# Fills of 6, 9 and 9 products, a priority for the recurrence's steps, and the embedding moved ahead of the last two pool units

## The chip, the core and the metric

The kernel runs on one core of one Trainium2 chip. A core has a matmul engine (TensorE, in the profile PE, with PEld for its weight loads), a vector engine (DVE), a scalar engine (ACT), GpSimd (POOL) and SyncE (SP), which only issues DMA transfers here. Each engine works through its own list of instructions in order; semaphores tie the lists together. Transfers are issued by SP and ACT and run beside the engines. The metric is the time of one execution on the device, in microseconds (us).

## The reference

One layer of a decoder with 512 tokens and a width of 2048, in float32. Half of the width is a linear recurrence (RWKV-7, 16 heads of 64), the other half causal means over trailing windows of 2, 4, 8 and 16 tokens. The code is cut to what is computed; `token_shift` delays by one token.

```python
h = rms_norm(x, norm_g[i])
z = jnp.einsum('btd,dn->btn', h, w_in[i])
# columns of z: r, k, v, two low-rank inputs, gate of the heads, pool input u, gate of the pool
zs = zs + (token_shift(zs) - zs) * mu[i]
...
def step(S, inp):                      # the recurrence, token by token, for each head
    sa = jnp.einsum('bhvk,bhk->bhv', S, -kk_t)
    S = (S * w_t[:, :, None, :]
         + sa[..., None] * (kk_t * a_t)[:, :, None, :]
         + v_t[..., None] * k_t[:, :, None, :])
    y_t = jnp.einsum('bhvk,bhk->bhv', S, r_t)
    return S, y_t
...
y = head_group_norm(y, ln_w[i], ln_b[i])
y_rwkv = (y + bonus.reshape(B, T, D_RWKV)).astype(dt) * jax.nn.silu(g_rwkv)
d = causal_multiscale_pool(u).astype(dt)
y_pool = jnp.einsum('btgc,gcd->btgd', d, w_pool[i]).reshape(B, T, D_POOL)
y_pool = y_pool * pool_scale[i] * jax.nn.silu(g_pool)
x = x + jnp.einsum('btc,cd->btd', jnp.concatenate([y_rwkv, y_pool], axis=-1), w_out[i])
gate = jax.nn.sigmoid(jnp.einsum('btd,de->bte', x, w_pg[i]) + b_pg[i])
x = x + gate * jnp.einsum('btq,qd->btd', p[i], w_ple[i])
return rms_norm(x, final_g)
```

## The kernel before

**Precision and products.** Every large product is made of three: each operand is split into a high and a low part (L132, L133 for weights: ACT casts the high part, DVE subtracts to get the low one), and `mm3` issues high by high, high by low, low by high. A "product" below is one instruction with 512 columns.

**Stages.** Up to about 50 us x is normalised and transposed into `hhi`, `hlo`. Then, to about 712 us, eight pairs of heads (j = 0 to 7) are worked through by `recur(j)`. Until 750 us what is left of the filler runs out, then come the product with w_out (`acc_o`) and, from about 930 us, the one with w_pg (`acc_g`).

**A pair of heads.** `recur(j)` goes over 8 chunks of 64 tokens. A chunk is a chain of three steps, called hops here. In *py*, PE multiplies by the state `sbd`, and DVE adds into `zs` (L773). In *pu*, PE multiplies by `zs`, and ACT copies the result into `uv` in two halves (L781). In *ps*, PE multiplies by `uv`, and DVE writes the next state `sbd` in two halves (L790 in the first chunk, L792 behind it); POOL makes `s0p` from it. Each hop waits for the one ahead, so PE needs other work in between.

**The filler.** That work is a generator, `stream()`, over the list `jobs`: the columns k, r, v and g of the next pair (48 products each), 16 pool units (`pool_unit(n)`, 48 products `zb` each; units with n mod 4 of 0 or 1 make windowed sums by DVE, L409 to L413, the others a gate and the map `wp` of 6 products, `pp`), and the embedding p by w_ple (`embed_unit`, four of 24 products, `pple`; ACT copies each result into `ple` and stores it to `pled`, from where `recall` loads it later). `pump(n)` draws at least n products: the generator yields 3 at a time, and what was drawn too much is carried over in `debt`. Between hops stand `pump(HC1)`, `pump(HC2)`, `pump(HC3)` of 8 products each, so that with steps of three the fills come as 9, 9 and 6 in turn. In the first chunk `between()` draws 16 products, computes the scores of the next pair (`pbo`, `pm`) and draws 16 more. Behind the eight chunks `finish` (transposes `pyt`, gate, store of `yo` to `yd`) is put off into the next pair's `gather`; for the last pair it runs behind `pump(HE)` at the end. `load_y` reads `yd` back as `yin` and splits it into `yhi`, `ylo` for w_out, in the order 8 to 13, 0 to 7, 14, 15.

**What sets the order.** PE's order is that of the program text (`keep_in_program_order`) up to the end of the filler. On the other engines a scheduler orders the instructions by priority, which is the place in the program unless it is raised. Buffers come from pools in turn: an instruction that writes a tile waits until the last reader of that buffer is done, for `ple` until the store to `pled` has landed.

In head 7 the filler in the hops is pool units (the last drawn there is the beginning of unit 15), and the embedding stands at the end of `jobs`, behind unit 15.

## Time and profile before

| | us |
|---|---|
| time, median of 3 runs | 1123.82 (1123.53 to 1124.64) |
| the profiled execution | 1124.23 |
| its span | 1122.5 |
| PE busy in the span | 1080.7 |
| mean granted clock | 0.994 of full |

How to read it: a row of the timeline gives the start, the duration, the engine, the line, the operation with output and inputs, the shape, how many such instructions in a row, and in brackets how long the engine stood idle ahead of it and what released it. A row of the waits gives the engine, the tile and the line that waited, what it waited for, then the total, how often and the longest. Matmuls are pipelined and their ends are modelled, so that rows of PE overlap. Durations of all other engines are measured. The letters q and ld behind an engine (ACTq, SPq, PEld) are its issue of DMAs and its weight loads.

### The profile page before, as it was taken

To read this page: it belongs to the slowest core of one execution; us is meant where nothing else is said; L and a number is where in the kernel's file an instruction comes from. 1 tells how busy PE (TensorE), PEld (TensorE's weight loads), DVE (VectorE), ACT (ScalarE), POOL (GpSimd) and SP (SyncE) were. 2 spreads that over 40 slices of the span, in tenths; PEclk is the share of its full clock that TensorE was granted. 3 is DMA by queue.
4 is the path that set the end of the run, shared out by engine and by line. 5 is a ranking of instruction groups with operands and counts; after the bars stand their busy time and mean duration, and the time that the engine had idled before them with its cause. 6 is when DMAs were issued, how large, how long until landed. Compare 5 with 4: busy or idle time off the path is not lost.

```text
span 1122.5 us, 17255 instructions
## 1 busy us (share of the span) xinstructions
PE 1080.7 (96%) x6090; PEld 881.0 (78%) x6090; DVE 707.8 (63%) x1835; ACT 450.1 (40%) x917; POOL 68.5 (6%) x180
## 2 busy tenths in 40 slices
PE   5999999999999999999999999979999999999996
PEld 4888887877877877878778787857888888888885
DVE  6677868778679688687886946534424423345265
ACT  7633435335335244353352433453222222233246
POOL 2100110110010000200101002000000000000000
PEclk9999999999999999999999999989999999999998
DMA  7433333332423333324234342486434437354444
GB/s 227 118 90 96 103 102 78 104 92 73 122 75 103 101 85 91 98 68 113 76 98 118 88 119 66 133 282 231 161 101 162 139 125 226 112 188 147 143 132 150
DMA packets 178357, 138.56 MB, mean 123 GB/s; under 512 B 34549, under 2 KB 139614, under 8 KB 178270
## 3 DMA queue, kind: packets, MB, share of 16 engines
q1 hardware_dynamic: 158270, 104.94, 31.7%
q10 hardware_dynamic: 20000, 32.52, 9.0%
q8 instruction: 48, 0.79, 0.3%
q14 instruction: 39, 0.32, 0.1%
HBM read 118.02 MB, written 18.87 MB: 122 GB/s over the span
## 4 chain that ended last, share of the span: by engine, by line
PE 59%; DVE 8%; ACT 3%; DMA 3%; issue 2%; ACTq 0%; DVEq 0%
PE acc_o L156 15%; PE acc_g L156 14%; PE zb L156 12%; PE zg L156 4%; PE zk L156 4%; PE zr L156 2%; PE zv L156 2%; DMA pled<-ple 2%; PE py L156 1%; DVE xw L648 1%; DVE tm L644 1%; DMA yin<-yd 1%; PE pp L156 1%; PE pm L156 1%; PE pu L156 1%
## 5 line engine op out<-in xcount | busy, mean ns | idle before, releaser
L133 DVE TENSOR_TENSOR wlo_g<-raw_g,whi_g 128x512 fp32r<-128x512 f32 x88 | 59.4, 684 | 85.6 <-ACT whi_g L132 85.3
L156 PE MATMUL zb<-hhi,whi_b 128*128 128x512 f32 x256 | 108.0, 422 | 0.0
L133 DVE TENSOR_TENSOR wlo_o<-raw_o,whi_o 128x512 fp32r<-128x512 f32 x64 | 43.8, 691 | 98.3 <-ACT whi_o L132 97.7
L156 PE MATMUL acc_o<-whi_o,yhi 128*128 128x512 f32 x256 | 101.4, 396 | 4.2 <-issue 4.1
L132 ACT CAST whi_g<-raw_g 128x512 fp32r<-128x512 f32 x88 | 54.4, 621 | 117.9 <-PE acc_g L156 72.2
L156 PE MATMUL acc_o<-wlo_o,yhi 128*128 128x512 f32 x256 | 101.3, 396 | 0.4 <-DVE wlo_o L133 0.4
L156 PE MATMUL acc_o<-whi_o,ylo 128*128 128x512 f32 x256 | 101.2, 395 | 0.0
L156 PE MATMUL zb<-hhi,wlo_b 128*128 128x512 f32 x256 | 100.6, 393 | 0.0
L156 PE MATMUL zb<-hlo,whi_b 128*128 128x512 f32 x256 | 100.0, 390 | 0.0
L156 PE MATMUL acc_g<-whi_g,x2hi 128*128 128x512 f32 (+1 forms) x224 | 86.7, 387 | 0.0
L156 PE MATMUL acc_g<-wlo_g,x2hi 128*128 128x512 f32 (+1 forms) x224 | 86.3, 385 | 0.0
L156 PE MATMUL acc_g<-whi_g,x2lo 128*128 128x512 f32 x224 | 86.0, 386 | 0.0
L132 ACT CAST whi_o<-raw_o 128x512 fp32r<-128x512 f32 x64 | 39.7, 623 | 104.0 <-PE acc_o L156 97.9
L132 ACT CAST whi_b<-raw_b 128x512 fp32r<-128x512 f32 x64 | 39.7, 620 | 79.5 <-PE zv L156 34.5
L799 POOL TENSOR_SCALAR s0p<-sbd,pw 64x64 f32<-64x64 f32 x96 | 49.2, 513 | 341.7 <-DVE sbd L792 256.4
L133 DVE TENSOR_TENSOR wlo_b<-raw_b,whi_b 128x512 fp32r<-128x512 f32 x64 | 43.8, 686 | 34.2 <-ACT whi_b L132 31.6
L156 PEld LDWEIGHTS acc_o<-whi_o,yhi 128*128 128x128 f32 x256 | 48.7, 190 | 14.9 <-issue 4.5
L156 PEld LDWEIGHTS acc_o<-wlo_o,yhi 128*128 128x128 f32 x256 | 48.7, 190 | 11.8 <-DVE wlo_o L133 1.6
L156 PEld LDWEIGHTS zb<-hhi,wlo_b 128*128 128x128 f32 x256 | 48.0, 188 | 11.2
L156 PEld LDWEIGHTS acc_o<-whi_o,ylo 128*128 128x128 f32 x256 | 48.8, 191 | 9.9
L648 DVE TENSOR_TENSOR xw<-xw,tm 128x60 f32<-128x60 f32 (+24 forms) x248 | 52.0, 210 | 6.8
L156 PEld LDWEIGHTS zb<-hhi,whi_b 128*128 128x128 f32 x256 | 48.3, 189 | 8.5
(283 smaller groups left out, 2541.6 us busy)
## 6 DMA issues: line engine op xcount, KB each, us to landing
raw_b<-in_w_in_dram SPq DMA_DIRECT2D x64, 256.0 KB
raw_o<-in_w_out_dram SPq DMA_DIRECT2D x64, 256.0 KB
raw_g<-in_w_pg_dram SPq DMA_DIRECT2D x64, 256.0 KB
raw_k<-in_w_in_dram SPq DMA_DIRECT2D x32, 256.0 KB
raw_r<-in_w_in_dram SPq DMA_DIRECT2D x32, 256.0 KB
raw_v<-in_w_in_dram SPq DMA_DIRECT2D x32, 256.0 KB
raw_g<-in_w_in_dram SPq DMA_DIRECT2D x32, 256.0 KB
n<-nd SPq DMA_DIRECT2D x16, 256.0 KB
```

Source lines behind the costliest of these rows:

```text
L132: nc.scalar.copy(hi, raw)
L133: nc.vector.tensor_tensor(lo, raw, hi.bitcast(F32), ALU.subtract)
L156: i = nc.tensor.matmul(*a, **k)
L644: nc.vector.tensor_tensor(tm[:, 0:n_, 0:w_], xin[:, 0:n_, s:s + 1].to_broadcast([P, n_, w_]), nb[s // 16][:, s % 16:s % 16 + 1, s + 1:32]. ...
L648: nc.vector.tensor_tensor(xw[:, 0:n_, s + 1:32], xw[:, 0:n_, s + 1:32], tm[:, 0:n_, 0:w_], ALU.add)
L799: nc.gpsimd.tensor_scalar(s0p[hc, :], nxt[hc, hc], pcn[hc], None, ALU.mult)
```

## The change

The sizes of the fills, the priorities, the places at which columns end, and the place of the embedding change; what is computed does not.

1. **Fills.** HC goes from (8, 8, 8) to (6, 9, 9): 6 behind py, 9 behind pu, 9 behind ps, each a multiple of the step of three.
2. **Priority.** The add into `zs`, the copies into `uv` and the updates of `sbd` are given to the scheduler with a priority raised by 1000 places.
3. **Where columns end.** `pump_to` replaces the second draw in `between()`: it draws about 16 products, more or fewer, so that the place in the current column (counted by `place`) is 0 or 9 modulo 24 there. H5 goes from 10 to 13 and HX from 16 to 13, both in `gather`. The last pair draws 9 in place of 16 in `between()`. The six products of a `wp` map are no longer counted (`yield 0`).
4. **Embedding.** The jobs "e" go from the end of the list to a place ahead of pool unit 14, and "p" (the transposes of p) ahead of unit 13. Each `ple` is a tile of its own with its own store (16 of 256 KB instead of 8 of 512 KB), in buffers that the pool's windowed sums use too (tags u and sw, two each); `phi` and `plo` move to other tags.

```diff
@@ -190,19 +190,18 @@
     nfill = [1, 1, 1, 1, 1, 1, 2, 8]
     jobs = [("z", nm, 0) for nm in "krvg"]
     n_ = 0
+    EC = 512
     for j in range(NJ):
         if j + 1 < NJ:
             jobs += [("z", nm, j + 1) for nm in "krv"]
         for i in range(nfill[j]):
-            jobs += [("p", None, 0)] if n_ + i == 14 else []
+
+            jobs += {13: [("p", None, 0)], 14: [("e", None, ec) for ec in range(D // EC)]}.get(n_ + i, [])
             jobs += [("b", None, n_ + i)]
         n_ += nfill[j]
         if j + 1 < NJ:
             jobs += [("z", "g", j + 1)]
-
-    EC = 512
     pled = dram.tile([T, D], F32, name="pled", bufs=1)
-    jobs += [("e", None, ec) for ec in range(D // EC)]
     plan_cols(O_L, "l")
     for kind, nm, j in jobs:
         if kind == "z":
@@ -386,12 +385,15 @@
 
     zt, dhl = {}, {}
 
+    place = [0]
+
     def zcols(ps, nm):
         for c in range(KT // CK):
             wh, wl = chunk(nm, c)
             for k in range(CK):
                 kk = c * CK + k
                 mm3(ps, wh[:, k, :], wl[:, k, :], hhi[:, kk, :], hlo[:, kk, :], kk == 0, kk == KT - 1)
+                place[0] = 3 * (kk + 1)
                 yield 3
 
     def pool_unit(n):
@@ -424,7 +426,7 @@
         wh, wl = chunk(f"wp{n}", 0)
         for k in range(2):
             mm3(pq, wh[:, k, :], wl[:, k, :], dh[:, k, :], dl[:, k, :], k == 0, k == 1)
-            yield 3
+            yield 0
         m = 2 * g + i
         nc.vector.scalar_tensor_tensor(sgp, pq, dp(73, m), sgp, ALU.mult, ALU.mult)
         nc.scalar.dma_start(out=yd[NJ + m], in_=sgp)
@@ -434,7 +436,6 @@
 
     def embed_unit(ec):
         ws = [chunk(f"e{ec}_{k}", 0) for k in range(2)]
-        outs = [pp.tile([P, 2, EC], F32, name=f"ple{ec}_{i}", tag=("dh", "dl")[i], bufs=1) for i in range(2)]
         for tt in range(NT):
             ts_ = slice(tt * P, (tt + 1) * P)
             pq = (psA, psM)[tt % 2].tile([P, EC], F32, name=f"pple{ec}_{tt}", tag=("acc", "m")[tt % 2])
@@ -446,11 +447,9 @@
                 mm(pq, plo[:, ts_], wh[:, 0, :], start=False, stop=k == 1)
                 if k == 0:
                     yield 3
-            t_ = outs[tt // 2]
-            nc.scalar.copy(t_[:, tt % 2, :], pq)
-            if tt % 2 == 1:
-                rows = slice((tt - 1) * P, (tt + 1) * P)
-                nc.scalar.dma_start(out=pled[rows, ec * EC:(ec + 1) * EC].rearrange("(t p) n -> p t n", p=P), in_=t_)
+            t_ = pp.tile([P, EC], F32, name=f"ple{ec}_{tt}", tag=("u", "sw")[tt % 2])
+            nc.scalar.copy(t_, pq)
+            nc.scalar.dma_start(out=pled[ts_, ec * EC:(ec + 1) * EC], in_=t_)
             yield 3
 
     def stream():
@@ -466,8 +465,8 @@
                     pt = psM.tile([P, T], F32, name=f"ppt{k}", tag="m")
                     for tt in range(NT):
                         tr(pt[:, tt * P:(tt + 1) * P], pn[0][:, tt, k * P:(k + 1) * P], ident)
-                    a_ = pp.tile([P, T], F32R, name=f"phi{k}", tag="u")
-                    b_ = pp.tile([P, T], F32R, name=f"plo{k}", tag="sw")
+                    a_ = rw.tile([P, T], F32R, name=f"phi{k}", tag=("sk", "sr")[k], bufs=2)
+                    b_ = rw.tile([P, T], F32R, name=f"plo{k}", tag=("sv", "sg")[k], bufs=2)
                     split(a_, b_, pt)
                     phl.append((a_, b_))
                 yield 3
@@ -493,6 +492,14 @@
                 return
             debt[0] -= c
 
+
+    def pump_to(n):
+        debt[0] += n
+        unit, half = sum(HC), HC[2]
+        off = (place[0] + debt[0]) % unit
+        debt[0] += min((-off, half - off, unit - off), key=abs)
+        pump(0)
+
     def need(nm, j):
         while (nm, j) not in zt:
             if next(big, None) is None:
@@ -501,7 +508,7 @@
 
     pws, kks, late = {}, {}, [None]
 
-    H1, H2, H3, H4, H5, HE = 6, 16, 16, 8, 10, 32
+    H1, H2, H3, H4, H5, HE = 6, 16, 16, 8, 13, 32
 
     def decay_and_rate(j):
 
@@ -770,7 +777,9 @@
             if ch > 0:
                 mm(py[:, sl], ar[:, q, 2 * par:2 * par + 2, :], cur, start=ch in (1, 4), stop=True,
                                  skip_group_check=True)
-                lead[0] = nc.vector.tensor_tensor(zs[pb:pb + 64], py[pb:pb + 64, sl], mv[pb:pb + 64, q, :], ALU.add)
+                with tc.high_priority(offset=HP):
+                    lead[0] = nc.vector.tensor_tensor(zs[pb:pb + 64], py[pb:pb + 64, sl], mv[pb:pb + 64, q, :],
+                                                      ALU.add)
                 step()
                 pump(HC1)
 
@@ -778,7 +787,8 @@
             mm(psu[:, 0:P], x1[:, 2 * q:2 * q + 2, :], zs, start=True, stop=True)
             for h in range(2):
                 hc = slice(64 * h, 64 * h + 64)
-                nc.scalar.copy(uv[pb:pb + 64, ch, hc], psu[hc, hc])
+                with tc.high_priority(offset=HP):
+                    nc.scalar.copy(uv[pb:pb + 64, ch, hc], psu[hc, hc])
             step()
             pump(HC2)
             if ch < NCH - 1:
@@ -786,11 +796,12 @@
                 mm(pss[:, 0:P], bkn[:, ch, :], uv[:, ch, :], start=True, stop=True)
                 for h in range(2):
                     hc = slice(64 * h, 64 * h + 64)
-                    if ch == 0:
-                        lead[0] = nc.vector.tensor_scalar(nxt[hc, hc], pss[hc, hc], pcc[hc], None, ALU.mult)
-                    else:
-                        lead[0] = nc.vector.scalar_tensor_tensor(nxt[hc, hc], pss[hc, hc], pcc[hc], s0p[hc, :],
-                                                                 ALU.mult, ALU.add)
+                    with tc.high_priority(offset=HP):
+                        if ch == 0:
+                            lead[0] = nc.vector.tensor_scalar(nxt[hc, hc], pss[hc, hc], pcc[hc], None, ALU.mult)
+                        else:
+                            lead[0] = nc.vector.scalar_tensor_tensor(nxt[hc, hc], pss[hc, hc], pcc[hc], s0p[hc, :],
+                                                                     ALU.mult, ALU.add)
                 s0p = rw.tile([P, C], F32, name=f"s0p{j}_{ch}", tag="s0p", bufs=2)
                 pcn = pw[:, ch + 1, C:C + 1]
                 if ch < NCH - 2:
@@ -850,8 +861,9 @@
 
         pending.append(finish)
 
-    HC, HT, HX = (8, 8, 8), 130, 16
+    HC, HT, HX = (6, 9, 9), 130, 13
     HS, HN = 9, 3
+    HP = 1000
     pending = []
     need("k", 0)
     need("r", 0)
@@ -869,10 +881,10 @@
     gather(0)
     for j in range(NJ):
         def between():
-            pump(H3)
+            pump(H3 if j + 1 < NJ else HC[2])
             if j + 1 < NJ:
                 scores(j + 1)
-                pump(H2)
+                pump_to(H2)
 
         if j + 1 == NJ:
             pn.append(rw.tile([P, NT, DPLE], F32, name="pn", tag="ar", bufs=2))
```

The first place is DVE in head 7, third chunk. `sw` and `u` are tiles of a pool unit's windowed sums, `wlo` the low part of filler weights, `sbd` the state, `zs` the input of pu. Before:

```order
L133 TENSOR_TENSOR wlo_b_3_4525<-raw_b_3_4522,whi_b_3_4524 128x512
L409 TENSOR_TENSOR sw_1_7548<-u_7546 128x511
L410 COPY sw_1_7548<-u_7546 128x1
L792 SCALAR_TENSOR_TENSOR sbd_567<-ps_2_7570,pw_6592,s0p_1_7516 64x64
L409 TENSOR_TENSOR sw_2_7551<-sw_1_7548 128x510
L410 COPY sw_2_7551<-sw_1_7548 128x2
L792 SCALAR_TENSOR_TENSOR sbd_567<-ps_2_7570,pw_6592,s0p_1_7516 64x64
L409 TENSOR_TENSOR sw_4_7554<-sw_2_7551 128x508
L410 COPY sw_4_7554<-sw_2_7551 128x4
L773 TENSOR_TENSOR zs_569<-py_0_7445,mv_7350 64x128
```

Now (the lines stand some ten further down in the text):

```order
L411 TENSOR_TENSOR sw_4_7548<-sw_2_7545 128x508
L412 COPY sw_4_7548<-sw_2_7545 128x4
L133 TENSOR_TENSOR wlo_e_0_0_4512<-raw_e_0_0_4509,whi_e_0_0_4511 128x512
L803 SCALAR_TENSOR_TENSOR sbd_567<-ps_2_7600,pw_6595,s0p_1_7531 64x64 x2
L411 TENSOR_TENSOR sw_8_7551<-sw_4_7548 128x504
L412 COPY sw_8_7551<-sw_4_7548 128x8
L414 TENSOR_TENSOR sw_8_7551<-sw_8_7551,rc_519 128x16
L415 SCALAR_TENSOR_TENSOR u_7540<-sw_8_7551,u_7540 128x512
L781 TENSOR_TENSOR zs_569<-py_0_7476,mv_7365 64x128
```

The two halves of the update stand together here, with no add of the pool between them. In heads 2, 4 and 6 one L133 stands between the halves in the new order, 17 times in all; before, 19 of the 56 updates are split, by one to four instructions.

The second place is ACT at the end of head 7, where `ysb` takes the last results of the recurrence out of PSUM. Before:

```order
L132 CAST whi_b_3_4708<-raw_b_3_4706 128x512
L430 DMA yd<-sgp_7768 128x512
L781 COPY uv_7296<-pu_7_7792 64x64
L132 CAST whi_wp_0_4737<-raw_wp_0_4735 128x256
L781 COPY uv_7296<-pu_7_7792 64x64
L813 COPY ysb_7444<-py_4_7630 64x256 x2
```

Now:

```order
L791 COPY uv_7318<-pu_7_7851 64x64 x2
L452 DMA pled<-ple_2_7826 128x512
L452 DMA pled<-ple_3_7836 128x512
L451 COPY ple_0_7848<-pple_0_7841 128x512
L451 COPY ple_1_7862<-pple_1_7855 128x512
L452 DMA pled<-ple_0_7848 128x512
L452 DMA pled<-ple_1_7862 128x512
L132 CAST whi_b_2_4736<-raw_b_2_4734 128x512
L132 CAST whi_b_3_4763<-raw_b_3_4761 128x512
L824 COPY ysb_7475<-py_4_7663 64x256 x2
```

Between the last `uv` and `ysb` stand now four stores, two copies of the embedding and two casts. On PE, the transposes `pyt` follow the last py by 39 products as before; behind them stand 78 products up to the first acc_o (18 of unit 14, its 6 of the map, 48 and 6 of unit 15), before it was 93 of the embedding.

The third place is ACT at the seam to w_out, where the weights of w_out are cast (`whi_o_8` is the first that PE needs, `whi_o_9` the second). Before:

```order
L900 DMA yin_8090<-yd 128x512
L453 DMA pled<-ple_1_8047 128x2x512
L900 DMA yin_8094<-yd 128x512
L137 CAST yhi<-yin_8090 128x512
L900 DMA yin_8098<-yd 128x512
L132 CAST whi_o_8_8139<-raw_o_8_8137 128x512
```

Now, some rows behind the cast of `whi_o_8`:

```order
L367 ACTIVATE sgp_8086<-zb_8037 128x512
L912 DMA yin_8114<-yd 128x512
L137 CAST yhi<-yin_8106 128x512
L137 CAST yhi<-yin_8110 128x512
L432 DMA yd<-sgp_8086 128x512
L137 CAST yhi<-yin_8114 128x512
L912 DMA yin_8118<-yd 128x512
L912 DMA yin_8122<-yd 128x512
L912 DMA yin_8126<-yd 128x512
L132 CAST whi_o_9_8173<-raw_o_9_8171 128x512
```

The cast of `whi_o_8` now stands ahead of unit 15's gate (`sgp`), that of `whi_o_9` behind it, behind the store of that gate, and behind a `yhi` whose `yin` is issued after the gate's tanh.

## The prediction

> **What bounds the kernel now.** I read the page's head first, then what the matmul engine waited for, then the timeline around the longest of those waits.
>
> ```profile
> span 1122.5 us, 17255 instructions
> PE 1080.7 (96%) x6090; PEld 881.0 (78%) x6090; DVE 707.8 (63%) x1835; ACT 450.1 (40%) x917; POOL 68.5 (6%) x180
> ```
>
> PE is busy in 96% of the span, no other engine in more than 63%. The count of products does not change, so the kernel can gain only where PE stands still or runs slowly. A busy share of 96% hides part of that, as the pitch of the products shows:
>
> ```profile
> 671.37 0.39 PE L156 MATMUL zb<-hhi,wlo_b 128*128 128x512 f32 x1
> 671.60 0.38 PE L156 MATMUL py<-sbd,ar 128*128 128x128 f32 x2
> ...
> 677.58 0.40 PE L156 MATMUL zb<-hhi,wlo_b 128*128 128x512 f32 x1
> 678.90 0.49 PE L156 MATMUL py<-sbd,ar 128*128 128x128 f32 x2 [0.93 <-DVE sbd L792]
> ```
>
> A row of 0.39 us is followed by the next after 0.23 us (671.37 to 671.60): rows overlap, and a 512-column product costs 0.23 us from start to start. Where py had to wait for the state (sbd), 1.32 us lie between the starts (677.58 to 678.90): 1.09 lost, of which the row names 0.93. So to each wait that a row names I add 0.16 us. Now the waits of PE from the prologue's end on:
>
> ```profile
> PE py L156 <- DVE sbd L792: 5.4, 8, 1.1
> PE acc_o L156 <- issue: 4.1, 1, 4.1
> ...
> PE pple L156 <- ACT ple L450: 2.5, 2, 1.6
> PE pm L156 <- DVE bk L592: 1.6, 3, 0.9
> PE pu L156 <- DVE zs L773: 0.9, 2, 0.7
> PE pp L156 <- ACT uv L678: 0.9, 1, 0.9
> PE pmv L156 <- ACT bkn L687: 0.9, 1, 0.9
> PE pss L156 <- ACT bkn L687: 0.8, 1, 0.8
> ...
> PE ps L156 <- ACT uv L781: 0.6, 1, 0.6
> ```
>
> Columns: total us, times, longest. Three groups. **Hops** (py, pu, ps): 5.4 + 0.9 + 0.6 = 6.9 in 11 waits, with 0.16 each 8.7 us. **Between the heads** (pm, pp, pmv, pss): 4.2 in 6 waits, so 5.2 us. **The seam** between the filler's end and w_out (pple, acc_o): 2.5 + 4.1 in 3 waits, so 7.1 us, and more, because PE then ran slowly:
>
> ```profile
> 745.72 0.39 PE L156 MATMUL pple<-whi_e,plo 128*128 128x512 f32 x1
> 750.26 0.77 PE L156 MATMUL acc_o<-whi_o,yhi 128*128 128x512 f32 x1 [4.15 <-issue]
> ...
> 756.31 0.57 PE L156 MATMUL acc_o<-wlo_o,yhi 128*128 128x512 f32 x1
> 756.72 0.40 PE L156 MATMUL acc_o<-whi_o,ylo 128*128 128x512 f32 x1
> ```
>
> From 750.26 to 756.72 stand 14 products; at 0.23 us they take 3.2 us, and they took 6.5, so 3.3 us went to the clock:
>
> ```profile
> 690.00:700.00 10.00, 9.04 (x47) 7.07 (x45) 8.21 (x20) 4.29 (x9) 2.56 (x3) 1.00 0.24 70
> 730.00:740.00 10.00, 7.82 (x34) 5.82 (x32) 3.88 (x6) 5.22 (x11) 0.00 (x0) 1.00 0.96 319
> 750.00:760.00 10.00, 9.74 (x29) 7.43 (x30) 4.95 (x8) 4.21 (x8) 0.00 (x0) 0.67 0.74 226
> ```
>
> Each row is a stretch: busy time and count of PE, PEld, DVE, ACT, POOL, then the granted clock, the DMA share, GB/s. The clock of 0.67 stands only behind the 4.15 us gap. The Trainium skill ("TensorE: Matmul & The Clock Gate", section "HAM oscillation — how this bites in real kernels") puts the point from which an idle gap halves the clock at about 3.4 us, and this row agrees with it on the one gap that it shows. The seam thus holds 7.1 + 3.3 = 10.4 us. All three groups together are 24.3 us: no gain of the change can exceed that by much.
>
> **What made the waits.** In a hop the state update is two DVE instructions, and DVE works in its listed order, whatever is ready:
>
> ```profile
> 690.59 0.69 DVE L133 TENSOR_TENSOR wlo_b<-raw_b,whi_b 128x512 fp32r<-128x512 f32 x1 [2.30 <-ACT whi_b L132]
> ...
> 691.99 0.28 DVE L792 SCALAR_TENSOR_TENSOR sbd<-ps,pw,s0p 64x64 f32<-64x64 f32 x1
> 692.19 0.67 DVE L409 TENSOR_TENSOR sw<-sw 128x510 f32<-128x510 f32 x1
> ...
> 692.97 0.29 DVE L792 SCALAR_TENSOR_TENSOR sbd<-ps,pw,s0p 64x64 f32<-64x64 f32 x1
> ...
> 694.09 0.28 DVE L773 TENSOR_TENSOR zs<-py,mv 64x128 f32<-64x128 f32 x1
> ```
>
> A pool add of 0.67 us stands between the halves, and the second comes 0.98 us after the first, where 0.2 us would do. PE's cover for that stretch is the fill, 9 products (2.0 us) or 6 (1.4 us), because a fill of 8 is drawn in steps of three. At the seam, ACT is the cause. Its copies of ple wait until an earlier pled transfer has landed and its buffer is free, and everything behind waits in order:
>
> ```profile
> 724.14 0.33 ACTq L849 DMA_DIRECT2D yd<-yo  x1
> 724.58 0.38 ACTq L453 DMA_DIRECT2D pled<-ple  x1
> ...
> 729.44 0.59 ACT L450 COPY ple<-pple 128x512 f32<-128x512 f32 x1 [1.16 <-DMA pled<-ple]
> 729.52 0.39 ACTq L453 DMA_DIRECT2D pled<-ple  x1
> 730.03 0.62 ACT L137 CAST yhi<-yin 128x512 fp32r<-128x512 f32 x1
> ...
> 735.74 0.59 ACT L450 COPY ple<-pple 128x512 f32<-128x512 f32 x1 [1.96 <-DMA pled<-ple]
> ...
> 749.02 0.62 ACT L137 CAST yhi<-yin 128x512 fp32r<-128x512 f32 x1 [1.85 <-DMA yin<-yd]
> 749.54 0.61 ACT L132 CAST whi_o<-raw_o 128x512 fp32r<-128x512 f32 x1
> ```
>
> The pled transfer issued at 724.58 let its buffer go at 729.44, 4.9 us later; the next took 6.2 us (729.52 to 735.74). The first weights of w_out were cast only at 749.54, so acc_o began at 750.26.
>
> **The change part by part.** *Hops.* In the new order every fill ahead of py and ps is nine, every one ahead of pu six; the priority takes the longer runs of pool adds out of the halves, though not all splits: one L133 (0.69 us) stays between them in heads 2, 4 and 6. Head 4 of before has the same, six times, in 431 to 508 us; PE's table for that stretch names one wait of py:
>
> ```profile
> PE py L156 <- DVE sbd L792: 0.5, 1, 0.5
> ```
>
> With 0.16 that is 0.7 us a head, 2.0 for three such heads. What is late next is pu, which now always has the short fill: zs (0.28 us) behind at most one instruction of 0.69 that runs already is about 1.0 to 1.3 us against 1.4, close to the edge in all 56 chunks. The two waits of pu (0.9 together) stood behind a backlog that the priority now passes; I leave 0.7 for it. **Gain 8.7 − 2.7 = 6.0** (1 to 8.7): at best all goes, at worst pu loses most of what py gains. Where the cover is gone by one L133 more, it costs 0.69 us in each chunk that has it.
>
> *Columns and the sections between heads.* H5 and HX only exchange three products; the wp products, no longer counted, put six more products (1.4 us) into one fill for each gated pool unit. Aligning the columns lets shifted outputs come due where a fill ends. The pm, pp, pmv and pss waits wait for DVE and ACT work whose place changes; nothing shows it directly, so from below nothing (new waits of the same kind, −2) to all of it (5.2). I take **2.0**, since the four waits have three different causes and the change names one.
>
> *Embedding in head 7.* Its 96 products leave the seam and 78 products of units 14 and 15 stand there instead, whose outputs need no landing to free a buffer. The four ple buffers are now single tiles, 16 stores of 256 KB instead of 8 of 512 KB: 8 more issues of 0.38 on ACT, 3.0 us beside an ACT that is busy 4.3 of 10 us there (row of 690). So the two pple waits, the 4.1 us gap and, with it, the slow clock go: 10.4 us. Three waits take their place. First, the transposes pyt of head 7: in the new order two pled issues and two weight casts stand ahead of the copy of ysb.
>
> ```profile
> 712.38 0.75 ACT L813 COPY ysb<-py 64x256 f32<-64x256 f32 x2 [1.59 <-PE py L156]
> ```
> ```profile
> 718.07 1.43 DVE L837 TENSOR_SCALAR ysb<-ysb,mvr,rs 128x64 f32<-128x64 f32 x6
> ```
> ```profile
> 721.24 0.60 PE L160 MATMUL pyt<-ident,ysb 128*128 128x128 f32 x4
> ```
>
> Before, ysb was finished at 719.50 and used at 721.24, 1.7 us to spare. Both casts wait for the last products of the chunk and take 0.62 each, then come the issues: ysb is about 3 us later, pyt waits about 1.4 us. Second, acc_o at its second k (weights whi_o_9): ACT casts them only behind unit 15's gate store and a yhi whose yin is issued after unit 15's tanh. A yin of 256 KB:
>
> ```profile
> 726.97 2.04 SPq L900 DMA_DIRECT2D yin<-yd  x3
> ```
>
> Issued at 726.97 and cast at 730.03, so 3.1 us. Counted from the last pp product: zb ends 6 products earlier (−1.4), tanh done and yin issued at about −0.4, yhi cast from 2.7 to 3.3, whi_o_9 until 4.0, its wlo 0.7 later; PE is there after 12 products, at 2.7. That is 1.6 us with this landing and 3.5 if it takes the 4.9 us of the pled store; I take 2.4. Third, whi_o_10, behind three more yin: 0.6 (0 to 1.5). Together 4.4, so **gain 10.4 − 4.4 = 6.0** (2 to 9).
>
> *Sum*: 6.0 + 2.0 + 6.0 = 14.0. Against the profiled execution, 1124.2 us (its span of 1122.5 plus 1.7 around it), 1110.2; the median of the runs is 0.4 below it, so **1110 us**.
>
> **The rivals.**
> (a) *The wait at whi_o_9 grows to a new slow clock.* The gap of 4.15 us did it, and no shorter one of the table did (1.6 did not). With landings as in 730 to 740 (share 0.96) the wait reaches 3.5. Price: 1.1 more for the wait and 3.3 for the clock, 1114.5. Against it: pled traffic is gone from there. By the Trainium skill's 3.4 us, an estimate, a wait of 2.4 keeps the clock and one of 3.5 loses it.
> (b) *The hops do not gain.* All pu hops now have the fill of six; if each of 56 loses 0.12 us, 6.7, and py the 2.0 above, that is the 8.7 of before, and the time 1116. For it: the short fill stands only there now, and halves stay split; against it: zs waits for one running instruction at most.
> (c) *Slower: ACT in head 7.* Each ple copy waits for the landing of the store four copies earlier; a chunk lasts about 6.2 us (from py at 671.60 to py at 678.90, without the 1.1 lost). While a store lands within that, nothing waits. If landing takes longer, the copy of uv stands behind the copy of ple on ACT, and ps waits on PE by the excess in each of four chunks, ysb and pyt after it. To eat the 14.0 and 2.2 us more the excess must be 4 us a chunk, a landing of 10 us; the longest shown of before was 6.2, at a DMA share of 0.96, and the share is 0.24 in 690 to 700. Price at that point: 1127.
> The Trainium skill ("DMA: Bandwidth & Descriptors", section "Anatomy of one DMA") gives about 2.0 us fixed for each DMA, and its section "Bandwidth" asks for 1 MiB and more in each; by these two, an estimate, 8 added stores cost 16 us where they go one after another, and the time would be 1126, on this rival's side. The three yin issued together at 726.97, the first of them cast 3.1 us later, rather show DMAs side by side; no run here has 256 KB stores of ple.
> (d) *The priority does not do what it says*: in the new order 17 of 56 updates are still split, 19 before. What goes is the longer run of pool adds, in head 7 above all. If the split itself makes the wait, (b) is what follows, so its chance is in (b).
>
> **How the numbers follow.** Forecast 0.55 (1104 to 1113.5); (a) 0.15; (b) 0.23; (c) 0.07. The forecast's low end is with hops and seam near their best: 8 + 3 + 9 = 20, 1104. The range reaches to (b) with its seam worse by 3: **1103 to 1119**; outside are (c) and the unlikely ends. A measurement of this kernel tells 0.2%, 2.2 us, from no change. Faster by that holds in the forecast, (a) and nearly all of (b): 0.90; within it, part of (b) and (c), 0.04; slower, most of (c), 0.06.
>
> **What would show it.** Hops right: the wait of py for sbd falls from 5.4 to under 2, and that of pu for zs stays under 2. Seam right: no gap above 3 us ahead of the first acc_o, clock 1.00 in every stretch of 10 us after 712, and the waits of pyt and of acc_o (for wlo_o or whi_o) in the table with 1 to 3 us. Wrong, if ps waits for uv in head 7, if the clock falls again behind whi_o_9, or if the time moves in the stages before 50 or after 770 us, where I expect nothing.

## The result, and the profile after

The changed kernel takes 1113.65 us (1113.49 to 1115.08), the kernel before 1124.23 us beside it: a ratio of 0.9905, with an interval of 0.9893 to 0.9916. That is 10.6 us less, inside the range (1103 to 1119), 3.7 us above the forecast and 0.9 below rival (a), 1114.5. The page's head after:

```profile
span 1112.0 us, 17260 instructions
PE 1076.4 (97%) x6090; PEld 879.9 (79%) x6090; DVE 709.1 (64%) x1835; ACT 449.7 (40%) x917; POOL 77.8 (7%) x180
```

The waits of PE after (tile and line, what it waited for, total us, times, longest):

```profile
PE acc_o L156 <- ACT whi_o L132: 6.8, 1, 6.8
...
PE pm L156 <- DVE bk L599: 2.3, 3, 1.5
PE pu L156 <- DVE zs L781: 1.1, 4, 0.4
PE pbk L160 <- ACT sig L526: 0.8, 2, 0.5
PE py L156 <- DVE sbd L803: 0.8, 3, 0.3
...
PE pyt L160 <- DVE ysb L848: 0.5, 1, 0.5
PE pp L156 <- ACT uv L685: 0.4, 1, 0.4
```

The waits of py fell from 5.4 to 0.8 us, those of pple are gone. The wait of 4.1 ahead of the first acc_o is gone too, but ahead of its second k (the 13th product) stands one of 6.8. What follows it is in the timeline of PE:

```profile
737.77 0.39 PE L156 MATMUL acc_o<-whi_o,ylo 128*128 128x512 f32 x1
744.94 2.08 PE L156 MATMUL acc_o<-whi_o,yhi 128*128 128x512 f32 x4 [6.78 <-ACT whi_o L132]
746.82 0.63 PE L156 MATMUL acc_o<-wlo_o,yhi 128*128 128x512 f32 x1
...
749.72 0.40 PE L156 MATMUL acc_o<-whi_o,ylo 128*128 128x512 f32 x1
```

and in the stretches of 10 us (busy time and count of PE, PEld, DVE, ACT, POOL, granted clock, DMA share, GB/s):

```profile
730.00:740.00 10.00, 8.16 (x37) 6.41 (x35) 5.47 (x9) 4.84 (x8) 0.00 (x0) 1.00 0.90 311
740.00:750.00 10.00, 5.06 (x13) 4.01 (x14) 6.33 (x10) 5.47 (x9) 0.00 (x0) 0.66 0.67 210
750.00:760.00 10.00, 10.00 (x46) 8.28 (x45) 6.24 (x10) 5.16 (x9) 0.00 (x0) 1.00 0.66 226
```

The gap is 737.77 to 744.94, 7.17 us from start to start, 6.9 more than the pitch. The rows behind it stand 0.43 us apart instead of 0.23. The clock of 0.66 is the mean of ten us; from 742.79 to 749.62 alone it was 0.50. The timeline of ACT shows why the second weights of w_out came so late:

```profile
735.35 0.62 ACT L137 CAST yhi<-yin 128x512 fp32r<-128x512 f32 x1 [1.72 <-DMA yin<-yd]
736.53 0.62 ACT L137 CAST yhi<-yin 128x512 fp32r<-128x512 f32 x1 [0.56 <-DMA yin<-yd]
737.54 0.62 ACT L137 CAST yhi<-yin 128x512 fp32r<-128x512 f32 x1 [0.38 <-DMA yin<-yd]
...
738.54 0.60 ACT L367 ACTIVATE sgp<-zb 128x512 f32<-128x512 f32 x1 [0.39 <-DMA raw_o<-in_w_out_dram]
738.91 0.33 ACTq L912 DMA_DIRECT2D yin<-yd  x1
741.20 1.31 ACT L137 CAST yhi<-yin 128x512 fp32r<-128x512 f32 x2 [2.06 <-DMA yin<-yd]
...
744.27 0.62 ACT L132 CAST whi_o<-raw_o 128x512 fp32r<-128x512 f32 x1 [1.13 <-DVE ylo L138]
```

The tanh of unit 15's gate could have run from about 734 on, when its `zb` was done (the last of it stands ahead of the six map products that end at 735.28). It ran at 738.54, because three `yhi` stood ahead of it, each waiting for a landing. The casts behind it waited for landings until 741.20, three more `yin` were issued, and only then, at 744.27, came the cast of the weights.

For the comparisons below I add up, from the starts of all rows of PE, the distance from each product to the next less its pitch (0.227 us for 512 columns, in proportion for fewer). "Recurrence" is that sum from 50 us to the last py of head 7, "hops" the part of it ahead of the py, pu and ps of the chunks (128 columns), "seam" what follows to the 72nd product of acc_o. Most of the recurrence's sum is small distances at every product that all kernels share; only differences count. (The expectations cut at 712 us instead, which gives 67.7 and 13.3 for the run with fills and priority.) "Before" was run beside each group on its chip; the ratios differ by up to 0.1% from the quotient of the two medians beside them, as they are taken over the executions. In the group with 1125.07 one execution of the kernel before ran at a clock of 0.656 and took 1533.28 us, and is left out of the ratios. The three sums are those of the one profiled execution of each kernel, which can differ from the median: 1126.55 us for "embedding moved only", 1125.08 for "fills only", within 0.8 of the median for the others.

| kernel | us | before | ratio, 95% interval | recurrence | hops | seam |
|---|---|---|---|---|---|---|
| before | 1124.23 | | | 69.6 | 10.6 | 12.6 |
| changed | 1113.65 | 1124.23 | 0.9905 (0.9893 to 0.9916) | 61.8 | 4.8 | 10.7 |
| fills only | 1123.75 | 1125.13 | 0.9989 (0.9979 to 0.9998) | 69.2 | 10.4 | 13.7 |
| priority only | 1121.93 | 1125.13 | 0.9968 (0.9957 to 0.9980) | 67.1 | 6.9 | 13.4 |
| fills and priority | 1122.37 | 1125.13 | 0.9969 (0.9956 to 0.9983) | 67.4 | 6.4 | 13.5 |
| + column places | 1120.74 | 1125.07 | 0.9964 (0.9950 to 0.9977) | 64.8 | 6.0 | 15.2 |
| + maps not counted | 1115.85 | 1125.07 | 0.9920 (0.9902 to 0.9938) | 63.7 | 5.2 | 10.3 |
| + 48 products up front | 1122.84 | 1125.49 | 0.9975 (0.9966 to 0.9985) | 70.1 | 8.5 | 11.7 |
| changed, embedding not moved | 1111.21 | 1124.04 | 0.9877 (0.9857 to 0.9896) | 61.5 | 4.4 | 8.3 |
| embedding moved only | 1124.05 | 1124.04 | 0.9994 (0.9983 to 1.0006) | 75.0 | 13.2 | 10.7 |
| changed, casts first | 1107.37 | 1124.04 | 0.9848 (0.9830 to 0.9866) | 61.7 | 4.7 | 2.4 |
| the same, loads later | 1104.70 | 1124.04 | 0.9822 (0.9805 to 0.9839) | 62.0 | 4.7 | 1.4 |
| the same, embedding not moved | 1106.31 | 1125.13 | 0.9829 (0.9813 to 0.9846) | 61.5 | 4.5 | 2.7 |
| casts first, loads later, fills 9, 6, 9 | 1105.99 | 1125.07 | 0.9833 (0.9817 to 0.9849) | 61.0 | 3.7 | 2.5 |

The three lines with a plus each add their one thing to fills and priority.

Of the 10.6 us that the change takes off, 5.8 are in the hops, 2.0 elsewhere in the recurrence and 1.9 at the seam. The other 0.9 lie mostly ahead of 50 us: the first product of `zl` starts at 16.75 us before and at 15.99 after, and anywhere between 15.65 and 16.64 in the other kernels, none of which changes anything there. By heads (each from the last py of one to that of the next), the recurrence's sum falls most in head 7, from 10.8 to 6.5 us.

### The profile page after: what moved, and what is told of

It reads as the page before. It is cut to its first block, busy times and chain, and to the rows that moved or that the text cites. A ratio compares the mean times of both kernels' runs of the same rounds, so it can differ in the third digit from the quotient of the medians.

```text
span 1112.0 us, 17260 instructions
## 1 busy us (share of the span) xinstructions
PE 1076.4 (97%) x6090; PEld 879.9 (79%) x6090; DVE 709.1 (64%) x1835; ACT 449.7 (40%) x917; POOL 77.8 (7%) x180
## 4 chain that ended last, share of the span: by engine, by line
PE 48%; ACT 2%; DMA 2%; DVE 1%; issue 0%; ACTq 0%; SPq 0%
PE acc_o L156 16%; PE acc_g L156 14%; PE zb L156 8%; PE pple L156 2%; DMA yin<-yd 1%; PE zr L156 1%; PE zg L156 1%; PE zv L156 1%; PE zk L156 1%; PE py L156 1%; PE px L992 1%; PE pu L156 1%; PE pp L156 1%; ACT L1039 0%; PE ps L156 0%; PE pm L156 0%
## 5 line engine op out<-in xcount | busy, mean ns | idle before, releaser
L133 DVE TENSOR_TENSOR wlo_g<-raw_g,whi_g 128x512 fp32r<-128x512 f32 x88 | 59.6, 685 | 86.2 <-ACT whi_g L132 84.4
L133 DVE TENSOR_TENSOR wlo_o<-raw_o,whi_o 128x512 fp32r<-128x512 f32 x64 | 43.9, 691 | 101.4 <-ACT whi_o L132 101.4
L810 POOL TENSOR_SCALAR s0p<-sbd,pw 64x64 f32<-64x64 f32 x96 | 55.9, 582 | 324.0 <-DVE sbd L803 257.7
L133 DVE TENSOR_TENSOR wlo_b<-raw_b,whi_b 128x512 fp32r<-128x512 f32 x64 | 43.7, 685 | 33.5 <-ACT whi_b L132 33.2
```

Source lines behind the costliest of these rows:

```text
L133: nc.vector.tensor_tensor(lo, raw, hi.bitcast(F32), ALU.subtract)
L810: nc.gpsimd.tensor_scalar(s0p[hc, :], nxt[hc, hc], pcn[hc], None, ALU.mult)
```

## The experiments

### Is it ACT's order at the seam? Casts first

```diff
@@ wsplit, in the changed kernel @@
+        if nm in ("o0_9", "o0_10", "o0_11"):
+            with tc.high_priority(offset=400):
+                nc.scalar.copy(hi, raw)
+                nc.vector.tensor_tensor(lo, raw, hi.bitcast(F32), ALU.subtract)
+            return hi, lo
```

> The changed kernel, with the casts of the second to fourth weights of w_out (o_9, o_10, o_11) given a higher priority, so that they stand ahead of unit 15's gate on ACT and not behind its store and a yhi that waits for a landing. Theory (ACT's order makes the 6.9 us gap, and the gap makes the slow clock behind it): the gap ahead of the second k of acc_o falls to under 1.5 us, the clock stays at 1.00 in 740 to 750, and the time falls by 8 to 9 us to about 1105. Rival (the yin and the weights land late, whatever the order): the wait moves to another yhi or weight, the gap stays above 3 us in sum, and the time falls by less than 3 us, to above 1110.5.

Measured: 1107.37 us, and the seam loses 2.4 instead of 10.7. No wait of acc_o above 0.3 us is left, and the stretch that was slow reads:

```profile
740.00:750.00 10.00, 9.69 (x42) 7.36 (x41) 5.37 (x9) 4.76 (x8) 0.00 (x0) 1.00 0.74 251
```

The transfers are the same, only three casts and their subtractions stand elsewhere: the gap is made by the order (ACT's casts, with DVE's subtractions behind them), and the slow clock goes with the gap. The time fell by 6.3 us against the changed kernel (other chip; by the two ratios 0.57%, 6.4 us), less than the 8 to 9 expected, with 8.3 us fewer lost at the seam; 1.4 us more are lost behind it, where two products of acc_o wait for DVE's `wlo_o` and lose 0.6 us each.

### Do the loads in the seam slow yin? Loads later

```diff
@@ on top of the casts first: recall and the load of x @@
-            nc.scalar.dma_start(out=t_, in_=pled[...])
+            with tc.issue_after(casts["o0_13"].ins):
+                nc.scalar.dma_start(out=t_, in_=pled[...])
...
-            nc.scalar.dma_start(out=t_, in_=x[rows, es])
+            with tc.issue_after(casts[f"o{ec}_13"].ins):
+                nc.scalar.dma_start(out=t_, in_=x[rows, es])
```

> The kernel of the casts put first, and the loads of x and of the stored embedding that stand in the seam (8 of 256 KB) held until acc_o's sixth k. Theory (order alone): within 1 us of the kernel with the casts first, about 1105. Rival (these loads slow the yin, 5.4 us from issue to cast in place of 3.1): 2 us or more below it, about 1103.

The loads of x for the three later quarters of w_out's columns are held in the same way. Measured: 1104.70 us, 2.7 less than with the casts first in the same group, so the rival of that expectation holds. The first `yin` of the seam, with the loads in the seam (SP's issue, then ACT's cast, from the casts first):

```profile
724.51 1.28 SPq L917 DMA_DIRECT2D yin<-yd  x3
```
```profile
730.16 0.62 ACT L142 CAST yhi<-yin 128x512 fp32r<-128x512 f32 x1 [3.81 <-DMA yin<-yd]
```

and with the loads later:

```profile
722.62 1.29 SPq L919 DMA_DIRECT2D yin<-yd  x3
```
```profile
725.46 0.62 ACT L144 CAST yhi<-yin 128x512 fp32r<-128x512 f32 x1 [1.29 <-DMA yin<-yd]
```

5.65 us against 2.84 for the same transfer. So the seam was made late by two things: the order on ACT, the larger one, and 2 MB of loads that nothing needs yet. How these loads slow the `yin` is not shown. Three of the eight, of `pler`, were issued within 1.5 us of it (724.53 to 725.96), and SP's loads of `raw_o` stand at other times too. It is not the DMA share: that was lower with the loads (0.54 in 724 to 726) than without them (0.73 and 0.93 in 722 to 726). This kernel has the lowest ratio of all, 0.9822 of before where the changed one is 0.9905; two further down lie within its interval.

### What does the move of the embedding give? Undone, and alone

The first run puts the jobs "e" and "p", the tiles and the stores of the embedding back as before, in the changed kernel; the second does only that part, in the kernel before.

```diff
-            jobs += {13: [("p", None, 0)], 14: [("e", None, ec) for ec in range(D // EC)]}.get(n_ + i, [])
+            jobs += [("p", None, 0)] if n_ + i == 14 else []
...
+    jobs += [("e", None, ec) for ec in range(D // EC)]
```

> The changed kernel with its embedding put back to the end, with tiles and stores as before; fills, priorities and column places stay. Theory (the gain comes from the hops and the sections between heads, the seam gives next to nothing): the hops lose about 5 us in place of 10.6, the seam shows the same pple waits and the 4.1 us gap as before, and the time is 1116 to 1117.5. Rival (the move also takes the pool adds out of head 7's hops and so makes a part of the hops' gain): head 7's py waits stay, and the time is 1119 or more.

> The kernel before with the move of the embedding alone (its place, tiles, stores and buffers); fills of 8, no priorities. Theory (the seam gives about 2 us by itself): about 1122, with a gap ahead of the second k of acc_o above 5 us and a slow clock behind it. Rival (head 7's hops gain from the move as well, 2.8 us of waits stood there): 1119 or less.

Undone: 1111.21 us, 2.4 us *faster* than the changed kernel (other chip; by the two ratios 0.28%, 3.1 us, and the intervals just overlap); the recurrence loses nearly the same, the seam 8.3 instead of 10.7. Theory and rival were both wrong, the theory right only on the hops (4.4): neither thought that the seam would gain without the move (12.6 before). Its pple waits are down to 0.2 us, and one gap is left:

```profile
738.18 0.39 PE L156 MATMUL acc_o<-whi_o,ylo 128*128 128x512 f32 x1
742.02 0.80 PE L156 MATMUL acc_o<-whi_o,yhi 128*128 128x512 f32 x1 [3.45 <-ACT whi_o L132]
```

Alone: no change (0.9994). The theory had the seam right: it gains 1.9 us, as in the changed kernel, with a gap of 5.61 us, ahead of the third k instead of the second, and a slow clock behind it. It did not have the recurrence, which loses 5.4 more in the profiled execution (2.5 us slower than the median), most of it in one place. The jobs "p" stand ahead of unit 13 now, so DVE's list in head 7 has two subtractions of `plo` among the pool adds, ahead of both halves of the state, and without the priority py waits for them all. DVE, then PE, then the stretch:

```profile
676.61 0.69 DVE L138 TENSOR_TENSOR plo<-ppt,phi 128x512 fp32r<-128x512 f32 x1
...
677.88 0.68 DVE L138 TENSOR_TENSOR plo<-ppt,phi 128x512 fp32r<-128x512 f32 x1
...
680.14 0.29 DVE L788 SCALAR_TENSOR_TENSOR sbd<-ps,pw,s0p 64x64 f32<-64x64 f32 x1
```

```profile
676.79 0.40 PE L156 MATMUL zb<-hhi,wlo_b 128*128 128x512 f32 x1
680.48 0.80 PE L156 MATMUL py<-sbd,ar 128*128 128x128 f32 x2 [3.30 <-DVE sbd L788]
```
```profile
680.00:690.00 10.00, 9.52 (x45) 7.74 (x46) 4.29 (x13) 3.00 (x7) 1.82 (x4) 0.67 0.09 27
```

That gap, too, ended in a clock of 0.67. The move, then, pays in neither place: alone it changes nothing, and in the changed kernel, where this wait is gone (its longest of py is 0.3 us), it costs 2.4 us as the seam stands. With the seam mended, the two come together:

> The kernel without the embedding's move, with the casts of w_out's weights first and the loads later, as in the best run so far. Theory (the move pays once the seam's order on ACT is mended, since the copies of ple no longer stand in the seam's queue): 1106 to 1108, 2 us above the same with the move. Rival (the move brings nothing in either order): within 0.7 us of it, about 1104.5.

1106.31 us, on another chip. The time is in the theory's range, but the ratios 0.9822 and 0.9829 lie only 0.8 us apart, and their intervals overlap by more than that. By them the rival is the nearer one; whether the move brings 1 us is open.

### What gives the hops' gain? Fills, priority, both

```diff
-    HC, HT, HX = (8, 8, 8), 130, 16
+    HC, HT, HX = (6, 9, 9), 130, 16
```

and, alone and together with it, the `tc.high_priority(offset=HP)` of the change around `zs`, `uv` and `sbd`.

> The kernel before with the fills (6, 9, 9) alone. Theory (the backlog on DVE makes the waits, and the fills only move them): py's waits fall with the long fill to about 4, pu's rise with the short one to as much, the hops still lose 9 to 11 us, the time is 1122 to 1125. Rival (the short fill ahead of py makes the waits): the hops lose 5 to 6 us, the time is 1118 to 1119.

> The kernel before with the priority alone, fills of 8. Theory (backlog): the hops lose 4 to 6 us in place of 10.6, the time is 1118 to 1119. Rival (the short fill ahead of py): the hops still lose 8 us or more, the time is 1121 or more.

> The kernel before with fills and priority, without column places and embedding. Theory (these two make the whole gain of the hops): the hops lose 4 to 5 us as in the changed kernel, the sections between heads and the seam are as before, the time is 1117 to 1118.5. Rival (the column places make a good part of the hops' gain): the hops lose 7 us or more, above 1120.

The fills alone are worth 0.1%: py's loss falls from 7.7 to 5.9 us, pu's rises from 1.8 to 4.1, as the theory had it. The priority alone takes 3.7 us out of the hops: with 6.9 left they stand between the theory (4 to 6) and its rival (8 or more), and the time falls by 0.3%, to the rival's (1121 or more). Both together do no better, and again the time is the rival's (above 1120): the hops lose 6.4, and the sections between the heads lose more (pbk 6.2 instead of 4.3, pyt 3.0 instead of 2.1). So fills and priority bring 0.3% of the 1.2% that the changed kernel gains without the embedding's move (0.9969 and 0.9877). The rest lies in the third part.

### Which piece of the third part? Column places, maps not counted

One run adds `pump_to`, H5 and HX to fills and priority, the other only this:

```diff
             mm3(pq, wh[:, k, :], wl[:, k, :], dh[:, k, :], dl[:, k, :], k == 0, k == 1)
-            yield 3
+            yield 0
```

> The kernel before with fills and priority, and the column places (pump_to, H5 13, HX 13); map products counted as before. Theory (places remove what fills and priority added: pyt and pbk waits, and the pu waits on columns' outputs): 50 to 712 us loses 62 in place of 67.7, the seam stays at 13, time 1116.5 to 1117.5. Rival (places need the maps uncounted, since six counted products shift the columns against the fills): 65 or more, time 1119.5 or more.

> The kernel before with fills and priority (1122.4 us, seam 13.3 us lost by the starts of PE's products), and the map products not counted. No column places, no other draw. Theory (how much filler is left at the seam decides what is lost there): the seam, now with fewer products of the embedding, loses about 4 us less, the stages up to 712 us lose as much as with fills and priority (67.7), time 1118. Rival (the column places give the seam's gain too): seam as with fills and priority, time 1121 to 1123.

The single digit is the largest part of the change: 1115.85 us, 0.9920 against 0.9969, about 5.5 us. The recurrence loses 3.7 us less and the seam 3.2 less; the theory named the seam and missed the recurrence. The column places alone take 2.6 us from the recurrence and give most of it back at the seam; their time, 1120.74, is that of their rival. Together, with the last pair's draw of 9, they take 5.9 us out of the recurrence (67.4 to 61.5, the changed kernel without the move), nearly their sum.

Not counting the maps does two things at once. A column is 48 products and the three fills of a chunk are 24, so by the program without the maps columns end at the same hop in every second chunk; six counted products move that by a quarter of a chunk at each map. And 48 products more are drawn in the recurrence, so that 36 instead of 84 of the embedding stand behind pyt. To part the two I drew 48 products more ahead of the first pair, with the maps counted:

```diff
-    HC, HT, HX = (6, 9, 9), 130, 16
+    HC, HT, HX = (6, 9, 9), 178, 16
```

> The kernel before with fills and priority, maps counted as before, and 48 more products (one column) drawn ahead of the first pair (HT 178 in place of 130), so that from there to the end of the recurrence as many products are left as with the maps not counted: 36 behind pyt, as there. Theory (not counting the maps helps in 50 to 712 because the columns keep their place against the fills; the seam gains because less of the embedding is left): the seam loses 10 to 11 us, 50 to 712 still 66.5 to 68, time about 1119.5. Rival (the 48 products drawn earlier bring the gain, wherever they come from): 50 to 712 loses 63 to 64 as with the maps not counted, time 1115.5 to 1116.5.

As much is left behind pyt as in the run with the maps not counted, and the seam loses 11.7 instead of 13.5. But the recurrence loses 70.1, not 63.7; the hops alone 8.5. Of this, 3.8 us stand in head 3, which loses 11.3 us where it loses 7.5 with fills and priority: a wait ahead of pyt and a slow clock behind it (shown in the last section). Without them about 66.3 would be left, still 2.6 more than with the maps not counted. So drawing 48 products early does not by itself bring the gain.

What does is open. A steady place of the columns is not what the traces show: from 300 us on, k, r and v of a pair end at the same place behind a hop in both runs, and that place changes from pair to pair in both. With the maps not counted it is 6 products behind py (308 to 334 us), 9 behind pu (380 to 406) and 9 behind ps (453 to 479), which are ends of fills; with fills and priority it is 6 behind pu, 3 behind py and 6 behind pu, short of the ends. But in the run of the column places all these columns end 9 behind pu or ps, at ends of fills, and its recurrence gains less. Of the 3.7 us, 3.9 lie in heads 5 to 7 and nothing on balance in the others.

### The short fill elsewhere

```diff
-    HC, HT, HX = (6, 9, 9), 130, 13
+    HC, HT, HX = (9, 6, 9), 130, 13
```

> The best kernel so far (embedding moved, casts first, loads later; 1104.7 us, hops lose 4.7), with fills (9, 6, 9): nine ahead of pu, six ahead of ps. Theory (pu's short fill is what is left in the hops; uv on ACT has no such backlog): pu's 3.0 us go, ps takes 0.5 to 1, the time is 1102 to 1103.5. Rival (ACT's queue is as full: ps then waits for uv by as much): 1104.5 or more.

pu's loss goes from 2.9 to 0.2 us and ps pays 0.4 for it, as the theory said; but py's goes from 1.7 to 3.1, with the same nine products ahead of it, and the seam's from 1.4 to 2.5. The time, by the ratios, is the same as without this (0.9833 to 0.9822). The time itself is the rival's (1104.5 or more), though not for the rival's reason, since ps hardly waits. The waits are not the short fill's alone.

## Why the prediction was right, and where it failed

**The bound.** PE's waits were what could be gained, and the ceiling of 24.3 us held: the best kernel here takes 19.3 us off in its group (1124.04 to 1104.70).

**The hops.** Forecast 6.0; the sum of the distances went from 10.6 to 4.8, 5.8 us. The named waits of py fell to 0.8, below the 2 that I named as the sign. The size was right, the reason was not, so that the number came out is luck: I credited fills and priority, which by themselves took 4.2 us out of the hops and added 2 us of waits between the heads. That pu would be the next to be late was right: 3.0 us of the 4.8 are pu's.

**Between the heads.** Forecast 2.0; the recurrence as a whole lost 7.8 us less, of it 5.8 in the hops, so 2.0. That is luck as well: the wait of pm, which I had counted among those to fall, grew from 1.6 to 2.3 us, while those of pp, pmv and pss fell from 2.6 to 0.4 or less. Here too I priced the wrong thing. I gave the third part of the change its 2.0 as a guess between bounds, and it carried 5.9 us of the recurrence and, through the amount left at the seam, more. The sentence that failed is the one on the maps, "six more products (1.4 us) into one fill": I counted their cover and not that they shift every column behind them.

**The seam.** Forecast a gain of 6.0, from 10.4 to 4.4; it gained 1.9, from 12.6 to 10.7 by the sums of the table. The four terms of what stays:
- pyt, forecast 1.4: 1.0 (0.7 and 0.3 from the starts of its two halves). Right in kind, a little smaller.
- whi_o_9, forecast 2.4 with a bound of 3.5: 6.9. This is the step that failed. I let the gate's tanh run as soon as unit 15's `zb` was done, at 1.4 us before the last map product, and counted one landing of yin behind it. In the trace it ran at 738.54, 3.3 us *behind* that product, because ACT, which works in its listed order, had three more `yhi` with landings ahead of it. I counted what stands between the tanh and the cast, and not what stands ahead of the tanh; the rows of the new order that I printed begin at the tanh.
- the clock, forecast to hold: 2.5 us lost to it (the 12 products from 744.94 on).
- whi_o_10, forecast 0.6: nothing, hidden behind the long wait.

**The rivals.** (a) came true, with a wait twice the 3.5 that it named. That the time is near its own (1113.65 and 1114.5) is luck in part: the wait was 3.4 us longer than in its price, but the seam before had lost 12.6 us and not 10.4. I had given it 0.15. The condition was wrong: I ruled landings as slow as in 730 to 740 out because the pled stores had left, and the loads of x and pler, 8 of 256 KB, had come in their place; holding these back gave 2.7 us. The DMA share by which I judged landings is no good measure of them, as the two `yin` above show. (b) did not come true in the changed kernel, though its parts did in the run of the fills alone. (c) did not: in the changed kernel's table of waits no ps stands, and no hop waits for ACT. Its price of 1127 is 1126.4 by its own terms (1124.2 and 2.2 more). The estimate with 2.0 us for each added store, which pointed to 1126, did not show either; the section it takes the figure from is on transfers that GpSimd issues, and ACT issues these. (d): with fills and priority alone 7 of the 56 updates are split and py loses 1.8 us, in the changed kernel 17 and py loses 1.7. So a split by one instruction is not by itself what makes py wait.

## What to carry to other kernels

An order printed for an engine is read from the instruction in question *backwards* to the last one that is sure to be free, each landing on the way counted; a chain that starts at "its input is ready" is too short on an engine that works in order. Where filler is drawn by count between the steps of a chain, the count itself is worth an experiment: six products a map, counted or not, moved more here than priorities and sizes did, and the reason that the program's order suggests did not hold in the traces. And a move that frees one stage is to be priced with the queue of the stage it moves from, since undoing this one gained 2.4 us (0.28% by the ratios).

## What the runs showed of the hardware

The granted clock fell after shorter gaps than I took for safe. In the run of the column places PE stood 2.42 us and then worked at half the clock for 3.41 us. First the row of PE, then stretches that begin and end where the clock changed or could have:

```profile
731.45 0.50 PE L156 MATMUL pple<-whi_e,phi 128*128 128x512 f32 x1 [2.42 <-ACT ple L453]
```
```profile
729.11:732.52 3.41, 1.07 (x5) 0.88 (x6) 1.90 (x3) 2.62 (x5) 0.00 (x0) 1.00 0.88 287
732.52:735.93 3.41, 3.41 (x9) 2.27 (x7) 0.00 (x0) 0.40 (x1) 0.00 (x0) 0.50 0.57 180
735.93:739.34 3.41, 2.78 (x12) 2.17 (x12) 1.39 (x2) 2.71 (x6) 0.00 (x0) 1.00 0.79 298
```

The fall sets in 1.07 us behind this gap's end, and in the changed kernel 2.15 us ahead of the end of its gap (742.79 and 744.94). The reason can be read from the traces: between 50 and 1090 us each slow stretch lasts 3.41 or 6.83 us, and where a run has several, their starts lie whole multiples of 3.41 us apart (360.26, 745.97 and 752.80 in the run with 48 products up front). So the clock is set on a fixed grid, and the idle time within one step of it decides, not the length of one gap. In the run just named two gaps with one transpose between them were enough:

```profile
359.18 0.30 PE L160 MATMUL pyt<-ident,ysb 128*128 128x128 f32 x1 [1.26 <-DVE ysb L841]
360.14 1.37 PE L160 MATMUL pyt<-ident,ysb 128*128 128x128 f32 x3 [0.66 <-DVE ysb L841]
```
```profile
356.85:360.26 3.41, 1.50 (x7) 0.83 (x5) 3.36 (x14) 0.71 (x2) 0.00 (x0) 1.00 0.31 85
360.26:363.67 3.41, 3.36 (x9) 2.35 (x10) 3.41 (x5) 0.78 (x1) 0.00 (x0) 0.50 0.26 77
```

PE is busy for 1.50 us of that step, so 1.91 us are idle. All 17 falls in these traces follow a step with at least 1.91 us of idle time, and no step at full clock with at most 1.67 us is followed by one; between the two figures there is no case. With the priority alone a gap of 4.33 us, which the grid cuts at 745.18 (1.67 and 2.66), cost one slow step; in the kernel without the embedding's move one of 3.45 us cost two.

The Trainium skill ("TensorE: Matmul & The Clock Gate", section "HAM oscillation — how this bites in real kernels") puts the point at about 3.4 us. The traces do not agree: single gaps of 2.42, 2.45 and 2.60 us cost the clock here, and single gaps of up to 1.67 us did not. A forecast that holds a wait of 2 us or more has to add a slow clock, and its price depends on where the grid lies: an estimate of 1.7 us for one step of work at half the clock (half of 3.41), and measured 2.5 in the changed kernel and 3.3 in the kernel before, both with two steps.
